# Who issues the transfers of the triangular inverses: a gated delta rule on one Trainium2 core

## The chip, the core and the metric

The kernel runs on one core of a Trainium2 chip. The metric is device microseconds (us) of that core for one execution. A NeuronCore has five engines that run side by side, each through its own queue of instructions in order: TensorE (PE in the rows, with PEld for its weight loads), VectorE (DVE), ScalarE (ACT), GpSimd (POOL) and SyncE (SP). An engine waits at the head of its queue until what the instruction needs is there, and all behind it waits too. A transfer (DMA) is issued by an instruction in the queue of one of the engines, here SyncE, ScalarE and, after the change, GpSimd; DMA engines beside them move the data.

## The reference, cut to what matters

A two-layer encoder trunk on 512 tokens of width 1024. Layer 0 mixes tokens by attention, layer 1 by a gated delta rule with eight heads; every layer has a SwiGLU block before and one behind. In the gated delta rule each head is cut into chunks, and for each chunk a unit lower triangular matrix has to be inverted:

```python
kb = k * beta[..., None]
l_mat = jnp.where(strict, jnp.einsum('bhncd,bhnsd->bhncs', kb, k) * decay, 0.0)
t_mat = lax.linalg.triangular_solve(l_mat + eye, jnp.broadcast_to(eye, l_mat.shape),
                                    left_side=True, lower=True, unit_diagonal=True)
u = jnp.einsum('bhncs,bhnsd->bhncd', t_mat, vb)
w = jnp.einsum('bhncs,bhnsd->bhncd', t_mat, kb * jnp.exp(gc)[..., None])
```

Then a scan over the chunks carries the state from one to the next.

## The kernel before, in words

All matrix work is float32, each large product as three matmuls of split operands (`wh`, `wl`: a weight panel's high and low part, `xnh`, `xnl`: the activations'). SyncE loads the weight panels, ScalarE makes `wh`, VectorE `wl`.

In the gated delta rule (`odd_mixer`, about 1330 to 1660 us of the execution) the eight heads go in four pairs. Here the chunks are 128 tokens wide, four of them. For each pair: projections to keys, queries and values (`gdn_proj`), on whose results a short convolution runs (`gdn_conv`: VectorE copies PSUM to `cx` at L924, ScalarE makes the first tap `cy` at L927, VectorE adds the other three at L929, ScalarE applies the activation, `c`); `gdn_keys` (stage `prep`) forms `iu`, the triangular matrix, at L980; `gdn_base` (stage `base`) inverts its 32x32 diagonal blocks; `gdn_head` (stage `scan`) joins these to the inverse of 128x128 and runs over the chunks; `gdn_gated` turns and gates the result `on`.

`gdn_base` is the part that the change touches. It takes a pair's two `iu` through DRAM (`iud`) so that every 32x32 block lands in one row of `lb` (four transfers, L1029), starts from the identity (`rr<-eye`, L1030), and does 31 elimination steps on GpSimd, each a product `tmp` (L1035) and a difference `rr` (L1038). Back through DRAM (`rd`, four transfers at L1041) the blocks land as `r` (two transfers, L1044). Each arrow waits for the one before: `lb` for both `iud`, the steps for all `lb`, `rd` for the last step, `r` for all `rd`. The first use of `r` is its transpose `t` on VectorE at L1053; the matmul `pb<-t,iu` on TensorE (L96) is the first that needs `t`, and it needs it of both heads.

GpSimd has one other job here: `rpow` (L160) computes small powers, `vs` in `gdn_keys` and `rs` at the end of a scan, where ScalarE's `on` (L1131) waits for it.

What stands on TensorE in which order is written by hand: `blend` merges a list of projections (the filler) with the stages, by the starts and pitches in `PLAN`, and `Ordered` keeps TensorE to the order so written. The order on the other engines is set by a scheduler that puts each instruction where it expects it to be ready.

Of the kernel before, what the change touches and what calls it, by code (L numbers as in the profile page):

```python
# [15 lines left out]
P = 128  # L16
# [85 lines left out]
class Trunk:  # L102
# [913 lines left out]
    def gdn_base(self, pool, G, Ks):  # L1016


        nc = self.nc
        n = BASE  # L1020
        iud = self.dram.tile([2 * HPITCH], F32, tag="iud", name="iud", bufs=2)
        for j, K in enumerate(Ks):
            nc.scalar.dma_start(self.rows_of(iud, j), K["iu"].rearrange("p (t s) -> p t s", s=P))
        lb = pool.tile([P, n, n], F32, tag="lb", name="lb", bufs=1)
        rr = pool.tile([P, n // 4, n], F32, tag="rr", name="rr", bufs=1)
        tmp = pool.tile([P, 9 * n], F32, tag="tmp", name="tmp", bufs=1)
        quarters = [slice(q * 2 * NBLK, (q + 1) * 2 * NBLK) for q in range(4)]
        for s in quarters:
            nc.scalar.dma_start(lb[s], self.blocks_of(iud))  # L1029
        nc.scalar.copy(out=rr, in_=G["eye"])  # L1030
        for j in range(n - 1):
            m, k = n - 1 - j, j // 4 + 1
            sh = [P, k, m]
            p = tmp[:, :k * m].rearrange("p (a b) -> p a b", b=m)
            nc.gpsimd.tensor_tensor(p, rr[:, :k, j:j + 1].broadcast_to(sh),  # L1035
                                    lb[:, j, j + 1:].rearrange("p (o m) -> p o m", o=1)
                                    .broadcast_to(sh), op=ALU.mult)
            nc.gpsimd.tensor_tensor(rr[:, :k, j + 1:], rr[:, :k, j + 1:], p, op=ALU.subtract)  # L1038
            yield
        for q, s in enumerate(quarters):  # L1040
            nc.scalar.dma_start(self.blocks_of(G["rd"], q, 4), rr[s])  # L1041
        for j, K in enumerate(Ks):
            K["r"] = pool.tile([P, T], F32, tag="r", name="r", bufs=3)
            nc.scalar.dma_start(K["r"].rearrange("p (t s) -> p t s", s=P), self.rows_of(G["rd"], j))  # L1044
        yield

    def gdn_head(self, pool, G, h, K):
# [154 lines left out]
```

## Time and profile before

| what | value |
|---|---|
| median of 3 runs | 2044.13 us (2042.98 to 2045.48) |
| the profiled execution's own time | 2044.75 us |
| its span, first to last instruction | 2042.9 us |
| mean granted clock of TensorE | 0.994 |
| busy: TensorE | 2011.8 us (98%) |
| busy: VectorE | 1086.6 us (53%) |
| busy: ScalarE | 747.5 us (37%) |
| busy: GpSimd | 129.6 us (6%) |

Times in the rows are microseconds from the span's start; "us in total, times, longest" belong to waits. A row of a timeline gives the start, the duration, the engine, the line and the operation as written <- read with its shape, and in brackets how long the engine sat idle before it and what ended that. The granted clock of TensorE is a share of full speed: 1.0 is 2.4 GHz, 0.5 is 1.2 GHz, and a value between is a mean over a stretch.

### The profile page before, as it was taken

The page shows a single profiled execution, that of the slowest core. Times are in us where ns is not written, and L with a number is a line of the kernel's source. Part 1 is how long each engine was busy: PE and PEld are TensorE (multiplying, and loading weights), DVE is VectorE, ACT ScalarE, POOL GpSimd, SP SyncE. Part 2 cuts the span into 40 slices and gives each one's busy share as a digit, 9 for nine tenths or more (in the row PEclk, how much of TensorE's full clock was granted, in tenths as well). Part 3 has the DMA queues.
Part 4 walks back from the last instruction along what each step waited for, and adds up shares of the span by engine and source line. Part 5 has one row for each costly group of instructions (what it writes and reads, how often), then busy time and mean ns, then how long its engine had stood idle before and what let it go on. Part 6 is the DMA issues. An engine that isn't in the chain of part 4 may idle for free.

```text
span 2042.9 us, 24836 instructions
## 1 busy us (share of the span) xinstructions
PE 2011.8 (98%) x9786; PEld 1669.5 (82%) x9786; DVE 1086.6 (53%) x1752; ACT 747.5 (37%) x1359; POOL 129.6 (6%) x294
## 2 busy tenths in 40 slices
PE   8999999999999999999999999998999999999998
PEld 7888888878888888888888888877877788888887
DVE  6442444587676443444544344477677675443543
ACT  5231233454663322323332123354455453322222
POOL 0000000000000000000000000005432400000000
PEclk9999999999999999999999999999999999999999
DMA  4332323222123233232332232334322333323232
GB/s 156 97 99 93 103 93 95 93 70 66 52 75 112 93 94 102 93 102 95 93 98 98 93 103 93 95 114 110 85 75 88 80 99 98 103 83 103 93 98 78
DMA packets 189866, 192.24 MB, mean 94 GB/s; under 512 B 28546, under 2 KB 165044, under 8 KB 189748
## 3 DMA queue, kind: packets, MB, share of 16 engines
q1 hardware_dynamic: 158916, 182.62, 28.5%
q10 hardware_dynamic: 30832, 8.02, 1.7%
q8 instruction: 77, 1.26, 0.3%
q14 instruction: 41, 0.34, 0.1%
HBM read 185.35 MB, written 5.26 MB: 93 GB/s over the span
## 4 chain that ended last, share of the span: by engine, by line
PE 89%; POOL 5%; DMA 2%; DVE 1%; issue 1%; ACT 1%; ACTq 0%; SPq 0%; POOLq 0%
PE mm L181 10%; PE mm L183 10%; PE mm L182 10%; PE pa L181 8%; PE pa L183 8%; PE pa L182 8%; PE pb L181 8%; PE pb L182 8%; PE pb L183 8%; PE mm L96 4%; POOL rr L1038 2%; POOL tmp L1035 2%; PE pb L96 1%; DMA lb<-iud 1%; DMA iud<-iu 1%
## 5 line engine op out<-in xcount | busy, mean ns | idle before, releaser
L175 DVE TENSOR_TENSOR wl<-raw,wh 128x1024 fp32r<-128x1024 f32 (+1 forms) x348 | 413.6, 1189 | 564.5 <-ACT wh L174 563.7
L174 ACT CAST wh<-raw 128x1024 fp32r<-128x1024 f32 (+1 forms) x348 | 355.4, 1021 | 707.5 <-PE pb L182 279.9
L181 PE MATMUL mm<-xnh,wh 128*128 128x512 f32 (+1 forms) x816 | 317.3, 390 | 0.6 <-ACT wh L174 0.6
L183 PE MATMUL mm<-xnh,wl 128*128 128x512 f32 (+1 forms) x816 | 317.8, 390 | 0.0
L182 PE MATMUL mm<-xnl,wh 128*128 128x512 f32 (+1 forms) x816 | 316.8, 389 | 0.0
L181 PEld LDWEIGHTS mm<-xnh,wh 128*128 128x128 f32 x816 | 153.9, 189 | 32.8 <-ACT wh L174 1.2
L183 PEld LDWEIGHTS mm<-xnh,wl 128*128 128x128 f32 x816 | 154.0, 189 | 32.0 <-issue 1.6
L182 PEld LDWEIGHTS mm<-xnl,wh 128*128 128x128 f32 x816 | 154.0, 189 | 30.6 <-issue 0.7
L181 PE MATMUL pa<-xnh,wh 128*128 128x512 f32 x400 | 156.3, 391 | 0.0
L183 PE MATMUL pa<-xnh,wl 128*128 128x512 f32 x400 | 155.8, 390 | 0.0
L183 PE MATMUL pb<-xnh,wl 128*128 128x512 f32 x400 | 155.8, 389 | 0.0
L181 PE MATMUL pb<-xnh,wh 128*128 128x512 f32 x400 | 155.8, 389 | 0.0
L182 PE MATMUL pb<-xnl,wh 128*128 128x512 f32 x400 | 155.8, 389 | 0.0
L182 PE MATMUL pa<-xnl,wh 128*128 128x512 f32 x400 | 155.8, 389 | 0.0
L226 ACT CAST hid<-hd 128x512 fp32r<-128x512 f32 x88 | 54.6, 620 | 209.1 <-DVE hd L398 209.1
L96 PE MATMUL mm<-xnh,wh 128*128 128x512 f32 x256 | 109.7, 428 | 11.5 <-DVE cx L924 11.5
L392 DVE TENSOR_TENSOR gr<-mm,rb 128x512 f32<-128x512 f32 x80 | 55.3, 691 | 94.7 <-PE mm L183 94.5
L182 PE MATMUL pb<-hid,wh 128*128 128x512 f32 x264 | 102.8, 389 | 0.0
L183 PE MATMUL pb<-hid,wl 128*128 128x512 f32 x264 | 102.8, 389 | 0.0
L181 PE MATMUL pa<-hid,wh 128*128 128x512 f32 x264 | 102.8, 389 | 0.0
L183 PE MATMUL pa<-hid,wl 128*128 128x512 f32 x264 | 102.8, 389 | 0.0
L181 PE MATMUL pb<-hid,wh 128*128 128x512 f32 x264 | 102.8, 389 | 0.0
(307 smaller groups left out, 3372.7 us busy)
## 6 DMA issues: line engine op xcount, KB each, us to landing
raw<-in_ffn_w_gate_dram SPq DMA_DIRECT2D x88, 512.0 KB, 3.6
raw<-in_ffn_w_up_dram SPq DMA_DIRECT2D x88, 512.0 KB, 3.5
raw<-in_ffn_w_down_dram SPq DMA_DIRECT2D x88, 512.0 KB, 3.6
raw<-in_gdn_w_in_dram SPq DMA_DIRECT2D x32, 512.0 KB, 3.9
raw<-in_att_w_in_dram SPq DMA_DIRECT2D x24, 512.0 KB, 3.5
raw<-in_gdn_w_out_dram SPq DMA_DIRECT2D x16, 256.0 KB, 2.7
xr<-in_x_dram SPq DMA_DIRECT2D x4, 512.0 KB, 5.4
raw<-in_att_w_out_dram SPq DMA_DIRECT2D x4, 512.0 KB, 3.3
```

What stands on the lines that cost most here:

```text
L96: return self.tc.keep_in_program_order(self.engine.matmul(*args, **kw))
L174: nc.scalar.copy(out=h[:, :n], in_=raw[:, :n])
L175: nc.vector.tensor_tensor(l[:, :n], raw[:, :n], h[:, :n].bitcast(F32), op=ALU.subtract)
L181: self.te.matmul(out, lhsT=lh, rhs=rh, start=start, stop=False)
L182: self.te.matmul(out, lhsT=lh, rhs=rl, start=False, stop=False)
L183: self.te.matmul(out, lhsT=ll, rhs=rh, start=False, stop=stop)
L226: nc.scalar.copy(out=h, in_=src)
L392: nc.vector.tensor_tensor(gr, g[j], self.rb, op=ALU.mult)
L1035: nc.gpsimd.tensor_tensor(p, rr[:, :k, j:j + 1].broadcast_to(sh), lb[:, j, j + 1:].rearrange("p (o m) -> p o m", o=1) .broadcast_to(sh), o ...
L1038: nc.gpsimd.tensor_tensor(rr[:, :k, j + 1:], rr[:, :k, j + 1:], p, op=ALU.subtract)
```

## The change

In `gdn_base` the four kinds of transfers are issued in GpSimd's queue instead of ScalarE's, and the copy of the identity runs on GpSimd. The two transfers that fill `rd` with zeros once, in the set-up, stay on ScalarE.

```diff
@@ -1020,14 +1020,14 @@
         n = BASE
         iud = self.dram.tile([2 * HPITCH], F32, tag="iud", name="iud", bufs=2)
         for j, K in enumerate(Ks):
-            nc.scalar.dma_start(self.rows_of(iud, j), K["iu"].rearrange("p (t s) -> p t s", s=P))
+            nc.gpsimd.dma_start(self.rows_of(iud, j), K["iu"].rearrange("p (t s) -> p t s", s=P))
...
         for s in quarters:
-            nc.scalar.dma_start(lb[s], self.blocks_of(iud))
-        nc.scalar.copy(out=rr, in_=G["eye"])
+            nc.gpsimd.dma_start(lb[s], self.blocks_of(iud))
+        nc.gpsimd.tensor_copy(rr, G["eye"])
...
         for q, s in enumerate(quarters):
-            nc.scalar.dma_start(self.blocks_of(G["rd"], q, 4), rr[s])
+            nc.gpsimd.dma_start(self.blocks_of(G["rd"], q, 4), rr[s])
         for j, K in enumerate(Ks):
             K["r"] = pool.tile([P, T], F32, tag="r", name="r", bufs=3)
-            nc.scalar.dma_start(K["r"].rearrange("p (t s) -> p t s", s=P), self.rows_of(G["rd"], j))
+            nc.gpsimd.dma_start(K["r"].rearrange("p (t s) -> p t s", s=P), self.rows_of(G["rd"], j))
```

The order of TensorE's and of SyncE's instructions stays the same, word for word. The other three change.

GpSimd, from the end of pair 0's inverse to the start of pair 1's (`vs` is the power in `gdn_keys` of pair 1; the rows with + are new):

```order
 L1035 TENSOR_TENSOR tmp<-rr,lb 128x8
 L1038 TENSOR_TENSOR rr<-rr,tmp 128x8
+L1041 DMA rd<-rr 32x8x32 x4
+L1044 DMA r<-rd 128x4x128 x2
+L1030 COPY rr<-eye 128x256
 L160 TENSOR_TENSOR vs<-sk,halfTrue 128x4 x2
+L1023 DMA iud<-iu 128x4x128 x2
+L1029 DMA lb<-iud 32x32x32 x4
 L1035 TENSOR_TENSOR tmp<-rr,lb 128x31
 L1038 TENSOR_TENSOR rr<-rr,tmp 128x31
```

All transfers of the inverse now stand between GpSimd's own instructions; for pair 1 the two `rs` of scan 0 stand between `rd` and `r`.

ScalarE, around the end of pair 0's inverse, before the change (`cy` and `c` are the convolution, `wh` a weight panel, `gosq` a sum of squares in `gdn_keys`):

```order
-L932 ACTIVATE c<-cy 128x512
-L1041 DMA rd<-rr 32x8x32 x4
-L927 ACTIVATE cy<-cx,conv 128x512
-L932 ACTIVATE c<-cy 128x512
-L174 CAST wh<-raw 128x1024
-L1044 DMA r<-rd 128x4x128 x2
-L1030 COPY rr<-eye 128x256
-L927 ACTIVATE cy<-cx,conv 128x512
-L960 ACTIVATE gosq,sk<-pa 128x128 x8
```

and what stands there now:

```order
+L932 ACTIVATE c<-cy 128x512 x2
+L927 ACTIVATE cy<-cx,conv 128x512
+L174 CAST wh<-raw 128x1024
+L927 ACTIVATE cy<-cx,conv 128x512
+L960 ACTIVATE gosq,sk<-pa 128x128 x4
```

The transfers are gone from between `c`, `cy` and `wh`.

GpSimd, in pair 3's inverse (`rs` belongs to scan 2):

```order
-L1035 TENSOR_TENSOR tmp<-rr,lb 128x48
+L160 TENSOR_TENSOR rs<-a_13064,halfFalse 128x4
+L1035 TENSOR_TENSOR tmp<-rr,lb 128x48
+L160 TENSOR_TENSOR rs<-a_13072,halfFalse 128x4
 L1038 TENSOR_TENSOR rr<-rr,tmp 128x6x8
```

The two `rs` stood thirteen steps of the inverse further down, between the last four.

## Rows read from the trace of the kernel before

**Rows 1.** The page's busy time (share of the span) and instructions of each engine.
```profile
PE 2011.8 (98%) x9786; PEld 1669.5 (82%) x9786; DVE 1086.6 (53%) x1752; ACT 747.5 (37%) x1359; POOL 129.6 (6%) x294
```
**Rows 2.** Waits of TensorE: us in total, times, longest.
```profile
PE mm L96 <- DVE cx L924: 11.5, 3, 6.1
```
**Rows 3.** Timeline of ScalarE, end of pair 0's inverse: start, us, engine, line, operation.
```profile
1424.98 1.82 ACTq L1041 DMA_DIRECT2D rd<-rr  x4
1426.89 0.72 ACT L927 ACTIVATE cy<-cx,conv 128x512 f32<-128x512 f32 x1 [11.63 <-issue]
...
1428.10 0.94 ACTq L1044 DMA_DIRECT2D r<-rd  x2
```
**Rows 4.** Timeline of ScalarE, end of pair 1's inverse.
```profile
1484.19 0.72 ACT L927 ACTIVATE cy<-cx,conv 128x512 f32<-128x512 f32 x1 [9.18 <-DMA rd<-rr]
```
**Rows 5.** Timeline of VectorE, behind pair 0's inverse.
```profile
1427.65 0.75 DVE L929 SCALAR_TENSOR_TENSOR cy<-cx,conv,cy 128x512 f32<-128x512 f32 x1 [8.69 <-ACT cy L927]
...
1433.23 0.71 DVE L1053 STREAM_TRANSPOSE t<-r 128x512 f32<-128x512 f32 x1
```
**Rows 6.** Timeline of TensorE, behind pair 0's inverse.
```profile
1429.06 0.80 PE L96 MATMUL mm<-xnh,wh 128*128 128x512 f32 x1 [6.12 <-DVE cx L924]
...
1434.30 0.39 PE L96 MATMUL mm<-xnh,wh 128*128 128x512 f32 x1
1434.53 0.39 PE L96 MATMUL mm<-xnl,wh 128*128 128x512 f32 x1
...
1438.50 0.89 PE L96 MATMUL pb<-t,iu 32*32 32x32 f32 x32
```
**Rows 7.** Timeline of TensorE, behind pair 1's inverse.
```profile
1487.53 0.80 PE L96 MATMUL mm<-xnh,wh 128*128 128x512 f32 x1 [4.83 <-DVE cx L924]
...
1491.54 0.95 PE L99 MATMUL pa<-ident,c 128*128 128x128 f32 x4
...
1497.87 0.89 PE L96 MATMUL pb<-t,iu 32*32 32x32 f32 x32
```
**Rows 8.** Windows: us, busy (instructions) of PE, PEld, DVE, ACT, POOL, clock, DMA, GB/s.
```profile
1422.90:1438.50 15.60, 9.48 (x31) 7.33 (x31) 10.01 (x23) 10.27 (x28) 4.07 (x9) 0.78 0.29 77
```
**Rows 9.** Timeline of TensorE, around the end of pair 3's inverse.
```profile
1617.51 1.25 PE L99 MATMUL pa<-ident,on 128*128 128x128 f32 x4 [2.54 <-ACT on L1131]
...
1628.45 0.89 PE L96 MATMUL pb<-t,iu 32*32 32x32 f32 x32
```
**Rows 10.** Timeline of GpSimd, near the end of pair 3's inverse.
```profile
1616.01 1.01 POOL L160 TENSOR_TENSOR rs<-a,halfFalse 128x4 f32<-128x4 f32 x1
1616.99 0.22 POOL L1038 TENSOR_TENSOR rr<-rr,tmp 128x16 f32<-128x16 f32 x1
```
**Rows 11.** Timeline of VectorE, the input of the first `rs` of rows 10.
```profile
1610.74 0.16 DVE L1127 SCALAR_TENSOR_TENSOR a<-gss,eq 128x4 f32<-128x4 f32 x1 [0.29 <-ACT gosr L1123]
```
**Rows 12.** Timeline of VectorE, the second transpose of pair 1.
```profile
1489.86 0.70 DVE L1053 STREAM_TRANSPOSE t<-r 128x512 f32<-128x512 f32 x1
```
**Rows 13.** Timelines of VectorE and TensorE, pair 2.
```profile
1550.19 0.71 DVE L1053 STREAM_TRANSPOSE t<-r 128x512 f32<-128x512 f32 x1 [0.31 <-DMA r<-rd]
...
1563.81 0.89 PE L96 MATMUL pb<-t,iu 32*32 32x32 f32 x32
```
**Rows 14.** Timeline of VectorE, both transposes of pair 3.
```profile
1625.71 1.30 DVE L1053 STREAM_TRANSPOSE t<-r 128x512 f32<-128x512 f32 x2
```
**Rows 15.** Timeline of ScalarE, start of pair 0's chain.
```profile
1383.53 0.37 ACTq L1023 DMA_DIRECT2D iud<-iu  x1
...
1385.90 2.48 ACTq L1029 DMA_DIRECT2D lb<-iud  x4
```
**Rows 16.** Groups by form, GpSimd: busy us, mean ns of one, idle before.
```profile
L160 POOL TENSOR_TENSOR rt<-ms,halfFalse 128x4 f32<-128x4 f32 x6 | 8.7, 1451 | 817.6 <-DVE ms L278 817.6
```
**Rows 17.** Windows (columns as in rows 8), pair 0's inverse in two parts.
```profile
1393.20:1419.00 25.80, 25.30 (x116) 20.70 (x115) 24.92 (x50) 14.77 (x38) 22.38 (x44) 1.00 0.40 120
1419.00:1425.00 6.00, 3.94 (x22) 3.01 (x20) 0.00 (x0) 0.00 (x0) 4.54 (x18) 1.00 0.05 17
```
**Rows 18.** Timeline of GpSimd, the first step of pair 0's inverse.
```profile
1393.25 0.56 POOL L1035 TENSOR_TENSOR tmp<-rr,lb 128x31 f32<-128x31 f32 x1 [14.79 <-DMA lb<-iud]
```

## The prediction, made before the changed kernel ran

> **What bounds the kernel now.** I read the busy shares first, then TensorE's waits, then the timelines of the engines around each wait, and last the granted clock of these stretches. TensorE is busy 2011.8 of 2042.9 us [rows 1], so only its waits, and stretches at a lower clock, can move the time. Its largest wait in the gated delta rule is for `cx`, 11.5 us in three times [rows 2]. Both long pieces of it have one cause, which the timelines show and the wait's own name does not. ScalarE issues the four `rd<-rr` transfers, which can't start until GpSimd has finished an inverse, and all that stands behind them on ScalarE stands still: before `cy` L927 it idles 11.63 us for pair 0 [rows 3] and 9.18 us for pair 1 [rows 4]. For pair 0 VectorE then idles 8.69 us before the next `cy` [rows 5], so `cx` is late and its PSUM bank is not emptied; TensorE idles 6.12 us up to 1429.06 [rows 6], and for pair 1 4.83 us up to 1487.53 [rows 7].
>
> Each wait has a second price. Twelve matmuls start between 1429.06 and 1434.30, 0.44 us apart, where the next two are 0.23 us apart [rows 6]; the granted clock of the stretch is 0.78 [rows 8], a mean of full speed (2.4 GHz) and of its half (1.2 GHz) behind the idle time. Lost: 5.24 - 12 x 0.23 = 2.5 us. After the second wait nine matmuls take 4.01 us instead of 2.07 [rows 7]; with the transposes behind them, which the half speed holds up by some 0.35 us (an estimate from their number), 2.3 us are lost.
>
> For pair 3 the wait is 2.54 us [rows 9]: the transposes of `on` need `rs`, which GpSimd runs at 1616.01 [rows 10] although its input `a` was written by 1610.90 [rows 11], since `rs` stands behind steps of the inverse in GpSimd's queue. With the same 2.3 us behind it this costs 4.8 us.
>
> **What the change removes.** No transfer of the inverse stands on ScalarE any more, so the first two waits for `cx` go: 6.12 + 2.5 and 4.83 + 2.3 us. The third goes too, 2.54 + 2.3 us, as `rs` moves thirteen steps of the inverse ahead. If nothing else were late, 21 us would be won. But the next thing on TensorE is late: `pb<-t,iu`, which needs the two transposed `r` of the pair, the end of the very chain that is moved. Without the old wait TensorE would come to it at
>
> - pair 0: 1438.50 - 8.6 = 1429.9, while the second `t` begins at 1433.23 and ends at 1433.9 [rows 5, 6];
> - pair 1: 1497.87 - 7.1 = 1490.8, while `t` ends at 1490.56 [rows 7, 12];
> - pair 2: 1563.81, while `t` ends at 1550.9: 12.9 us of slack [rows 13];
> - pair 3: 1628.45 - 4.8 = 1623.6, while `t` ends at 1627.0 [rows 9, 14].
>
> So even with transfers that cost GpSimd what they cost ScalarE, the waits partly move to `t`. From there each microsecond by which the chain from `iu` to `t` gets longer counts in full for pairs 0, 1 and 3.
>
> **What it adds to that chain.** Per pair, in series: the second `iud` issue, four of `lb`, the inverse, four of `rd`, two of `r`: eleven issues. On ScalarE they took 0.37 and 2.48 us [rows 15], 1.82 and 0.94 us [rows 3], together 5.6 us. No row shows a transfer issued by GpSimd. From below: GpSimd might hand one over in a tenth of a microsecond, and the chain would be 4.5 us shorter than now; nothing excludes that. At ScalarE's price it is as long as now. From above: a small instruction that GpSimd works through, `rs` on 128x4, takes 1.01 us [rows 10], and its costliest form `rt` 1.45 us [rows 16]. I take 1.0 us an issue, the nearest row on the engine that will do it: eleven issues are 11.0 us and the chain is 5.4 us longer (5.8 for pair 1, where the two `rs` stand between `rd` and `r` and run mostly while `rd` lands). With 1.45 us it is 10.4 us longer.
>
> The inverse itself also gets slower where VectorE stood idle beside it. From 1393.2 to 1419.0 VectorE was busy 24.92 of 25.80 us and 44 GpSimd instructions took 22.38 us, 0.51 us each; from 1419.0 to 1425.0, VectorE waiting, 18 took 4.54 us, 0.25 each [rows 17]. These are smaller steps too, so not all of it is contention. In the changed program VectorE works through the second stretch; at the first rate the 18 steps are 4.7 us dearer. I take 2 us for pair 0, 1 us for pair 1 (VectorE must have idled at the end of that inverse too, behind the same stop of ScalarE), none for pair 3.
>
> Hidden: the copy of the identity, about 0.5 us like the steps in [rows 17], runs while GpSimd waits for `lb` (14.79 us idle for pair 0 [rows 18]); were that cover gone it would cost its 0.5 us a pair. Behind the waiting `r` issues on GpSimd stand the copy, `vs` and the next pair's `iud`; the next `iu` comes from matmuls that stand behind `pb<-t,iu` in TensorE's order, so none of them is late. TensorE's and SyncE's orders don't change.
>
> **Sum.** New time of `pb<-t,iu`, with the slow matmuls behind the new wait (2.5 or 2.3 us), against now:
>
> - pair 0: 1433.9 + 5.4 + 2 + 2.5 - 1438.5 = +5.3 us
> - pair 1: 1490.6 + 5.8 + 1 + 2.3 - 1497.9 = +1.8 us
> - pair 2: the slack of 12.9 us holds 5.4 and two `rs` of 1.0; 0 us
> - pair 3: 1627.0 + 5.4 + 2.3 - 1628.45 = +6.2 us
>
> Together +13 us on the profiled execution's own 2044.75 us (span 2042.9 and 1.85 around it): 2057.8. The median of the runs shown lies 0.6 lower, at 2044.13: I predict 2057 us.
>
> **A rule weighed.** ScalarE loses far more by standing behind a transfer's wait than by issuing it: 11.63 us of idle time against 1.82 us of issue [rows 3]. The Trainium skill, "DMA: Bandwidth & Descriptors", section "Issuing engines are not separate DMA queues", says that starting transfers from several engines only saves the sequencer the time to start them, usually a small part. By that rule the change could win no more than those issues; by the row it wins the wait, if `t` is not late.
>
> **Rivals.**
>
> *A later start, no longer queue* (no difference). Issues overlap, and each of the four stages of the chain only starts a little later. Priced at 0.4 us a stage, about one `iud` issue of ScalarE [rows 15], the chain is 1.6 us longer: pair 0 +1.5; pair 1 1490.6 + 2.0 + 1 + 1.5 - 1497.9 = -2.8; pair 2 0; pair 3 1627.0 + 1.6 + 2 - 1628.45 = +2.2; sum +0.9, 2045 us. For it: a transfer's instruction may be handed on before its work is done. Against: in [rows 10] one instruction on GpSimd holds up the next. The Trainium skill, same page, section "Latency and other measured facts", gives about 1 us to the first byte on GpSimd's software path and 0.6 us on ScalarE's; no run here shows it yet, and an estimate from this page, 0.4 us more for each of four stages, would come to the same 2045 us.
>
> *GpSimd issues as cheaply as ScalarE* (faster). The chain is as long as now, and the place that wins is pair 1, where `t` then ends about when TensorE comes: pair 0 1433.9 + 2 + 2.5 - 1438.5 = -0.1; pair 1 1490.6 + 0.4 + 1 + 0.5 - 1497.9 = -5.4; pair 3 1627.0 + 1.5 - 1628.45 = 0; sum -6, 2038 us, and 2035 without contention. It decides from about 0.65 us an issue downward: there the sum crosses zero. For it: 11.63 and 9.18 us of idle time on ScalarE go for certain. Against: GpSimd's small rows.
>
> *Dearer than any row* (slower still). One `lb` issue covers 32x32 runs of 32 elements; if GpSimd's time goes by runs, an issue may be 2 us: 11 us more for each of three pairs, 2090 us.
>
> That ScalarE still stands is excluded by the new order, in which it has no transfer of the inverse.
>
> **How the numbers follow.** Forecast 0.55, dearer 0.07, later start 0.18, cheap issue 0.20. The range goes from the cheap case, 2037, to 1.45 us an issue (5 us more for three pairs), 2073. What a measurement of this kernel can tell from no change is about 0.2%, 4 us: faster 0.20, same 0.18, slower 0.62.
>
> **What would show it.** Right: ScalarE's idle times of 11.63 and 9.18 us and the `cx` waits of 6.1 and 4.8 us gone; in their place TensorE waiting for VectorE's `t` L1053, some 9, 8 and 9 us for pairs 0, 1 and 3, with a lower granted clock behind each; in GpSimd's queue transfers of about 1 us each, and 7 us or more from the last step of an inverse to the end of the second `r` issue. Wrong: issues of 0.5 us or less, or `t` in place when TensorE comes. If the part before the inverse is as long as now and only the `rd` and `r` part longer, the sum is some 6 us too high.

## The result

| | before | after |
|---|---|---|
| median of 6 runs each, on one chip | 2044.18 us (2042.95 to 2045.48) | 2056.43 us (2055.02 to 2061.3) |
| profiled execution | 2044.75 us, span 2042.9 | 2055.79 us, span 2054.0 |

The ratio is 1.006, with a 95% interval of 1.0049 to 1.0072: slower, by some 12 us. 2057 us was predicted. The sum came within a microsecond, but only one of its four terms did; that the errors of the others cancelled is luck.

### The profile page after: what moved, and what is told of

It is laid out like the page before. It is cut to its first block, busy times and chain, and to the rows that moved or that the text cites. A ratio compares the mean times of both kernels' runs of the same rounds, so it can differ in the third digit from the quotient of the medians.

```text
span 2054.0 us, 24865 instructions
## 1 busy us (share of the span) xinstructions
PE 2014.1 (98%) x9786; PEld 1671.5 (81%) x9786; DVE 1087.6 (53%) x1752; ACT 748.3 (36%) x1355; POOL 172.0 (8%) x346
## 4 chain that ended last, share of the span: by engine, by line
PE 89%; POOL 5%; DMA 2%; DVE 2%; issue 1%; ACT 1%; SPq 0%; POOLq 0%; ACTq 0%; DVEq 0%
PE mm L181 10%; PE mm L183 10%; PE mm L182 10%; PE pa L181 8%; PE pa L183 8%; PE pa L182 8%; PE pb L181 8%; PE pb L183 8%; PE pb L182 8%; PE mm L96 5%; POOL tmp L1035 2%; POOL rr L1038 2%; PE pb L96 2%; PE pb L615 1%; DVE cy L929 0%
## 5 line engine op out<-in xcount | busy, mean ns | idle before, releaser
L181 PE MATMUL pa<-hid,wh 128*128 128x512 f32 x264 | 102.7, 389 | 0.0
L182 PE MATMUL pa<-hid,wh 128*128 128x512 f32 x264 | 102.7, 389 | 0.0
```

The source lines that it names most:

```text
L181: self.te.matmul(out, lhsT=lh, rhs=rh, start=start, stop=False)
L182: self.te.matmul(out, lhsT=lh, rhs=rl, start=False, stop=False)
```

## The profile after, place by place

The page's busy time of the changed kernel answers to [rows 1]: TensorE has the same work, GpSimd 42 us more, of which the issues are most.

```profile
PE 2014.1 (98%) x9786; PEld 1671.5 (81%) x9786; DVE 1087.6 (53%) x1752; ACT 748.3 (36%) x1355; POOL 172.0 (8%) x346
```

TensorE's waits from 1340 to 1720 us (total, times, longest) answer to [rows 2]. The 11.5 us for `cx` are 1.4. What stands there instead is late for the inverse in one way or another:

```profile
PE pb L96 <- DVE kd L966: 7.9, 1, 7.9
PE pb L96 <- DVE t L1053: 7.0, 3, 5.3
PE pa L99 <- ACT vb L1013: 5.9, 1, 5.9
...
PE mm L96 <- DVE cx L923: 1.4, 1, 1.4
```

**Pair 0.** GpSimd's timeline answers to [rows 3], [rows 15] and [rows 18]: start, duration, operation, and in brackets the idle time before. The second `iud`, the four `lb`, the four `rd` and the two `r` take 0.77 + 3.15 + 2.35 + 1.54 = 7.8 us, where ScalarE took 5.6.

```profile
1383.59 0.77 POOL L1023 DMA_DIRECT2D iud<-iu  x1 [2.62 <-DVE iu L980]
1386.94 3.15 POOL L1029 DMA_DIRECT2D lb<-iud  x4 [2.58 <-DMA iud<-iu]
1394.69 0.23 POOL L1035 TENSOR_TENSOR tmp<-rr,lb 128x31 f32<-128x31 f32 x1 [4.60 <-DMA on<-gd]
...
1429.17 0.21 POOL L1038 TENSOR_TENSOR rr<-rr,tmp 128x8 f32<-128x8 f32 x1
1429.72 2.35 POOL L1041 DMA_DIRECT2D rd<-rr  x4 [0.34 <-POOL rr L1038]
1433.91 1.54 POOL L1044 DMA_DIRECT2D r<-rd  x2 [1.84 <-DMA rd<-rr]
1435.45 0.41 POOL L1030 COPY rr<-eye 128x256 f32<-128x256 f32 x1
```

VectorE and TensorE there (answering to [rows 5] and [rows 6]) stand before that result, each at the head of its own queue. TensorE's last projection begins at 1429.58, and it stops at 1437.84 - 7.88 = 1429.96; VectorE has stopped at 1427.71.

```profile
1437.08 0.71 DVE L1053 STREAM_TRANSPOSE t<-r 128x512 f32<-128x512 f32 x1 [9.37 <-DMA r<-rd]
1437.71 0.12 DVE L966 TENSOR_TENSOR kd<-br,kdc 128x4 f32<-128x4 f32 x1
...
1438.88 0.70 DVE L1053 STREAM_TRANSPOSE t<-r 128x512 f32<-128x512 f32 x1
```

```profile
1437.84 0.87 PE L96 MATMUL pb<-t,iu 32*32 32x32 f32 x16 [7.88 <-DVE kd L966]
1439.64 0.87 PE L96 MATMUL pb<-t,iu 32*32 32x32 f32 x16 [0.93 <-DVE t L1053]
```

The releaser named for the first is `kd`, a small instruction that ran directly behind `t` on VectorE; the wait is for `t`.

**Pair 1.** Not `t` but `vb` is what TensorE waits for. The chain reads from VectorE to GpSimd, ScalarE and TensorE: `a` is ready at 1482.85, but `rs` stands behind the inverse and the `rd` issues in GpSimd's queue, `on` waits for `rs`, and `vb` stands behind `on` on ScalarE. By the time TensorE reaches `pb<-t,iu`, at 1501.87, `t` is there: the second one ends at 1500.13 (answers to [rows 7] and [rows 12]).

```profile
1482.61 0.24 DVE L1127 SCALAR_TENSOR_TENSOR a<-gss,eq 128x4 f32<-128x4 f32 x1
...
1492.50 2.04 POOL L160 TENSOR_TENSOR rs<-a,halfFalse 128x4 f32<-128x4 f32 x2
...
1493.57 1.28 ACT L1131 ACTIVATE on<-on,rs 128x128 f32<-128x128 f32 x4 [5.62 <-POOL rs L160]
1494.76 1.11 ACT L1013 ACTIVATE vb<-pa,vs 128x128 f32<-128x128 f32 x4
...
1495.92 1.11 PE L99 MATMUL pa<-ident,c 128*128 128x128 f32 x4 [5.89 <-ACT vb L1013]
...
1501.87 0.89 PE L96 MATMUL pb<-t,iu 32*32 32x32 f32 x32
```

**Pair 2** wins 2.0 us that nobody had counted. In the kernel before, TensorE's transposes of `on` look like this (1.21 us for four; from the first to the next projection 0.96):

```profile
1549.39 1.21 PE L99 MATMUL pa<-ident,on 128*128 128x128 f32 x4 [0.23 <-ACT on L1131]
1550.35 0.48 PE L96 MATMUL mm<-xnh,wh 128*128 128x512 f32 x1
```

and in the changed kernel, where ScalarE no longer idles 8.04 us for `rd` ahead of them, like this:

```profile
1553.03 0.60 PE L99 MATMUL pa<-ident,on 128*128 128x128 f32 x4
1553.39 0.48 PE L96 MATMUL mm<-xnh,wh 128*128 128x512 f32 x1
```

Before, the four transposes take as long as ScalarE needs for four pieces of `on` (1.28 us for the four of pair 1): they follow it piece by piece. That the row is twice as long is not the clock: from 1549.4 to 1551.5 it is 1.00. Such a wait hardly counts as idle time (0.23 us here) and shows in the duration of a row.

**Pair 3.** GpSimd runs the two `rs` earlier (1613.93, against [rows 10]), the wait before `on` of [rows 9] is gone, and TensorE comes to `pb<-t,iu` at 1626.48, long before `t` ([rows 14]). The window's columns are those of [rows 8].

```profile
1631.82 0.87 PE L96 MATMUL pb<-t,iu 32*32 32x32 f32 x16 [5.34 <-DVE t L1053]
1633.37 0.87 PE L96 MATMUL pb<-t,iu 32*32 32x32 f32 x16 [0.68 <-DVE t L1053]
...
1648.08 0.73 PE L96 MATMUL pb<-vb,kdec 128*128 128x128 f32 x4
```

```profile
1628.00:1648.00 20.00, 15.50 (x131) 12.27 (x132) 5.28 (x13) 2.38 (x7) 1.33 (x2) 0.58 0.14 41
```

The clock of this row, 0.58, is a mean: 0.91 to 1632, while TensorE mostly stands, and 0.50 (1.2 GHz) in each quarter from there to 1648, 16 us behind the wait. From `pb<-t,iu` to the first `pb<-vb,kdec` it is 16.26 us, 15.58 of them busy; before, 1637.35 - 1628.45 = 8.90, all busy and at full clock.

How far the changed kernel is behind, by the same matmul in both traces:

| landmark on TensorE | before | after | behind | by this pair |
|---|---|---|---|---|
| `pb<-state,c`, scan of pair 0 | 1458.00 | 1460.45 | +2.45 | +2.45 |
| `pa<-ident,on` behind pair 1's start | 1515.75 | 1519.79 | +4.04 | +1.6 |
| `pb<-t,iu`, pair 2 | 1563.81 | 1565.88 | +2.07 | -2.0 |
| `pa` L274, behind the layer | 1690.76 | 1701.61 | +10.85 | +8.8 |

## The experiments

Twelve kernels, each timed in five rounds beside the kernel before (2044.3 to 2044.7 us in these sets). Unless said otherwise the edit is to the changed kernel, at 2056.4.

### Which pair loses

```diff
# gdn_base(..., p): own = p < 3
+        io = nc.gpsimd if own else nc.scalar      # for iud, lb, rd, r
+        nc.gpsimd.tensor_copy(rr, G["eye"]) if own else nc.scalar.copy(out=rr, in_=G["eye"])
```

> The changed kernel for pairs 0 to 2 alone; pair 3's transfers and its copy are ScalarE's again. Theory (pair 3's own chain, 27.55 us of inverse and a dearer chain around it, costs 8.8 us there): that goes, 2056.4 - 8.8 = about 2047.6 us, with the wait for t at 2.5 us or less in pair 3 and full clock from 1640 us on. Rival (pair 3's loss comes from what the pairs before it left, a later start of its inverse): 2054 to 2056 us. Second rival (ScalarE's own stop behind rd in pair 3, which only the old order hid): slower than 2056 us.

Measured: 2046.83 us, ratio to before 1.0015 (1.0006 to 1.0024). The theory holds: pair 3 makes 9.6 of the 12 us. Its `rs` are late again, TensorE waits 2.56 us before `on`, and then not at all for `t`; the stretch from 1628 has full clock.

```profile
1621.52 1.35 PE L99 MATMUL pa<-ident,on 128*128 128x128 f32 x4 [2.56 <-ACT on L1133]
```

```profile
1628.00:1648.00 20.00, 19.84 (x194) 16.31 (x193) 10.48 (x28) 6.65 (x24) 0.00 (x0) 1.00 0.21 57
```

So the early wait before `on`, which the prediction booked as a loss to be won back, goes with a `t` that is in time. This edit gives pair 3 both the old order and the old issues; which of the two decides is seen from `iud` and `lb` alone on ScalarE, further down. The early wait stood among projections of 512 columns and the clock was full again by 1628; the new wait stands before matmuls of 32 and 64 columns, with three projections at a time between them.

Pair 2 alone on GpSimd, with the same edit but for one line:

```diff
-        own = p < 3
+        own = p == 2
```

> The kernel before, with the transfers and the copy of pair 2 alone on GpSimd. Theory (pair 2 has 12.9 us of slack in its chain and loses ScalarE's stop of 8 us behind rd; between the ends of pair 1 and pair 2 the changed kernel won 2.0 us): about 2042 us. Rival (the 2.0 us were won back from what pair 1 had lost, not from pair 2's own edit): 2044 us, no difference. Second rival (issues on GpSimd hold up the inverse or rs of pair 2, so that the queues of pair 3 are late): 2047 us or more.

Measured: 2042.51 us, ratio 0.9996 (0.9987 to 1.0004): no difference that can be told. The trace shows the gain where the theory has it (from pair 1's `pb<-t,iu` to pair 2's 64.07 us, against 65.94 before). In the profiled execution, at 2046.68 us, more than that was lost on either side: from pair 0's `pb<-t,iu` to pair 1's 61.65 us (59.37 before), from pair 2's to pair 3's 66.77 (64.64). Whether the other runs keep part of the gain stays open.

### Which half of the chain, and the copy

```diff
-            nc.gpsimd.dma_start(self.rows_of(iud, j), ...)     # lb likewise
+            nc.scalar.dma_start(self.rows_of(iud, j), ...)
-        nc.gpsimd.tensor_copy(rr, G["eye"])
+        nc.scalar.copy(out=rr, in_=G["eye"])
```

> The changed kernel, with the first half of the chain (iud, lb, the copy of the identity) issued by ScalarE again; rd and r stay on GpSimd. Theory (the chain from iu to t sets the end, so every microsecond of issue and landing counts): in the changed kernel GpSimd issues one iud and four lb in 0.79 + 3.15 us, ScalarE did it in 0.37 + 2.48, and the landings were 0.4 + 0.3 us shorter; the first step of each inverse starts some 1.8 us earlier, pairs 0, 1 and 3 win it, 2056.4 - 5 = about 2051 us. Rival (only what stands behind the inverse matters, the first half is hidden): first steps of the inverse earlier or not, 2056 us. Second rival (ScalarE stands still again behind iud's landing, and what it makes for TensorE is late): 2058 us or more.

Measured: 2050.16 us, as the theory has it, but not for its reason. Pair 0's `pb<-t,iu` comes 1.4 us earlier, pair 1's 3.2 us later (TensorE waits 8.8 us for `vb`); what is won is pair 3's, as the table below shows. ScalarE stands still again, though no transfer that waits for the inverse is on it: the copy may not write `rr` before `rd` has been read out of it.

```profile
1431.77 0.40 ACT L1030 COPY rr<-eye 128x256 f32<-128x256 f32 x1 [12.16 <-DMA rd<-rr]
```

The same without the copy, which stays on GpSimd:

```diff
-            nc.gpsimd.dma_start(self.rows_of(iud, j), ...)
+            nc.scalar.dma_start(self.rows_of(iud, j), ...)
-            nc.gpsimd.dma_start(lb[s], self.blocks_of(iud))
+            nc.scalar.dma_start(lb[s], self.blocks_of(iud))
```

> The changed kernel, with iud and lb alone issued by ScalarE again; the copy, rd and r stay on GpSimd. With the copy on ScalarE too, the time was 2050.2 us, but the copy stood still for 12.16 us in pair 0 and 8.51 us in pair 1. Theory (the first half of the chain is some 1.8 us cheaper on ScalarE in each of three pairs): about 2051 us, with the wait for vb of pair 1 back at 4 to 6 us and that for t of pair 0 at 6 to 7. Rival (the copy's stop cost as much again in that run): 2046 us or less. Second rival (the copy's stop did no harm, and the gain of that run was the stop's, which delayed TensorE less than t does): 2056 us.

Measured: 2047.79 us, ratio 1.0018 (1.0009 to 1.0027). 8.6 us are won, more than the theory, less than the first rival, and the theory's price of 1.8 us a pair falls: the first step of pair 0's inverse is 0.94 us earlier (1393.75), its `pb<-t,iu` only 0.2 (1437.64). Nearly all of the gain is in pair 3, where the scheduler now puts `rs` two steps from the end of the inverse again (1618.71) and TensorE waits 2.55 us before `on`, not for `t`. The second `t` ends at 1629.62 + 1.48 = 1631.10 and `pb<-t,iu` begins at 1631.16: although `rd` and `r` stay on GpSimd, the early wait is just long enough. Pair 2's gain is gone: from pair 1's `pb<-t,iu` to pair 2's it is 66.10 us, with `rs` behind the inverse and the `rd` issues on GpSimd (1549.49) and `on` waiting 6.04 us for it. The kernels with one half of the chain on GpSimd and the other on ScalarE, or with `rd` and `r` on SyncE, all take 65.9 us or more here; 64.0 to 64.1 is seen only where both halves of pair 2 are on GpSimd.

The other half back on ScalarE:

```diff
-            nc.gpsimd.dma_start(self.blocks_of(G["rd"], q, 4), rr[s])     # r likewise
+            nc.scalar.dma_start(self.blocks_of(G["rd"], q, 4), rr[s])
```

> The changed kernel, with the second half of the chain (rd and r) issued by ScalarE again; iud, lb and the copy of the identity stay on GpSimd. Theory (ScalarE stands still behind rd in pairs 0 and 1, and a longer first half starts every inverse some 1.8 us later): ScalarE's idle times of some 12 and 9 us and the waits for cx of 6.1 and 4.8 us are back, each 1.8 us longer for pair 0; about 2044.2 + 1.8 + 1.8 + 1.8 = 2049 us. Rival (the first half is the cheap part, the second half makes the loss): 2044 us, as before. Second rival (both halves cost, each as dear as the whole): 2056 us.

Measured: 2054.40 us; the theory fails by 5 us. ScalarE idles 9.38 us in pair 0, as it said, but the waits for `cx` come to no more than 2.1 and 1.7 us, and pair 0 is 2.5 us better than in the changed kernel (`pb<-t,iu` at 1435.34). Pair 3 has the same loss as the changed kernel (a wait for `t` of 4.25 us), which the theory had not charged to the first half.

The copy alone, moved in the kernel before:

```diff
-        nc.scalar.copy(out=rr, in_=G["eye"])
+        nc.gpsimd.tensor_copy(rr, G["eye"])
```

> The kernel before, with the copy of the identity alone on GpSimd; all transfers stay on ScalarE. Theory (rd still stands ahead of cy on ScalarE): the idle times of some 11.6 and 9.2 us stay, no difference, 2044 us. Rival (the copy, not rd, is what holds ScalarE): they go, and the time falls to 2036 us or less. Second rival (the copy on GpSimd is in the chain): 0.4 us for each of three pairs, 2045.5 us.

Measured: 2044.34 us, ratio 1.0001 (0.9992 to 1.001), with ScalarE's 11.6 us before `cy` as they were. Copy and `rd` are two ways into one stop.

Over all kernels with the old table one number sorts pair 3, the time on TensorE from its first `pb<-t,iu` to `pa` L274:

| kernel | wait ahead of scan 3 | to `pa` L274 |
|---|---|---|
| before; pairs 0 to 2; pair 2 alone; `iud`, `lb` on ScalarE, with and without the copy; copy alone; `rd`, `r` on SyncE, with and without the copy (below) | `on`, 2.54 to 2.57 us | 62.30 to 62.35 us |
| changed | `t`, 5.34 | 69.79 |
| `rd`, `r` on ScalarE | `t`, 4.25 | 71.34 |
| `rs` on VectorE (below) | `t`, 3.98 | 69.98 |
| `lb` in eight (below) | `t`, 8.19 | 69.49 |

The span begins behind the wait: that TensorE waits there at all, 4 us or 8, costs 7 us or more after it.

### What an issue costs

`lb` in eight transfers of half the partitions each:

```diff
-            nc.gpsimd.dma_start(lb[s], self.blocks_of(iud))
+            for o in (0, NBLK):                     # half: 16 blocks of the 32
+                nc.gpsimd.dma_start(lb[s.start + o:s.start + o + NBLK], half)
```

> The changed kernel, with lb of each pair filled by eight transfers of half the partitions instead of four, all on GpSimd; the bytes are the same. Theory (an issue occupies GpSimd for about 0.79 us whatever its size, and the chain sets the end in pairs 0, 1 and 3): four issues more, 3.2 us a pair, 2056.4 + 9 = about 2065 us. Rival (an issue's time goes by its pieces, 1024 here, 512 then): the eight take as long as the four, 3.15 us, and the time is 2056 us. Second rival (the issue is hidden behind the landing of the transfer before): eight issues of 0.79, but the first step of the inverse no later than 1 us, 2058 us.

Measured: 2075.64 us, ratio 1.0156 (1.0142 to 1.017): 19 us slower, twice the theory. GpSimd's timeline of pair 0:

```profile
1383.50 2.55 POOL L1033 DMA_DIRECT2D lb<-iud  x4 [2.88 <-DMA iud<-iu]
1386.04 0.79 POOL L1023 DMA_DIRECT2D iud<-iu  x1
1389.93 2.52 POOL L1033 DMA_DIRECT2D lb<-iud  x4 [3.11 <-DMA iud<-iu]
1398.91 0.24 POOL L1039 TENSOR_TENSOR tmp<-rr,lb 128x31 f32<-128x31 f32 x1 [6.46 <-DMA lb<-iud]
```

An issue of half the size takes 0.64 us, not 0.79, so eight take 5.1 us against 3.15; the price is partly per issue, partly per piece. In pair 0 order comes on top: the second `iud` now stands behind four `lb` that wait for the first, and the inverse starts 4.2 us later. That the chain sets the end is borne out there: pair 0's `pb<-t,iu` is 5.4 us later, after a wait of 11.8. Pair 1's is 5.0 us behind the changed kernel's, pair 2's 10.3 and pair 3's 20.0 (it waits 8.19 us for `t`); in the scan of pair 2 the clock falls to 0.50 from 1583 to 1590, behind another wait of 2.16 us. How the last 15 us divide into chain, order and clock stays open.

### `rs` off GpSimd

```diff
-        self.rpow(rs, a2, NB)
+        nc.vector.reciprocal(rs, a2)
```

> The changed kernel, with rs made by VectorE as 1/a2, which leaves out the root; so GpSimd has only vs and the inverse. Theory (in pair 1 TensorE waits 5.89 us for vb, which stands behind on, which waits for rs, which stands behind the inverse in GpSimd's queue): that wait goes, TensorE comes to pb<-t,iu some 6 us earlier and waits there for t, which is only about 0.5 us earlier; pair 1 wins 1.5 us, pair 3, whose inverse holds two rs of about 1 us, wins 2: about 2053 us. Rival (the whole of the wait and the half clock behind it is won, t is not late): 2046 us. Second rival (rs has no part in it): 2056 us, and the wait for vb stays at 5.9 us.

Measured: 2058.70 us, 2 us slower than the changed kernel (this kernel leaves out the root in `rs`). The wait for `vb` is gone, so its cause is shown, and `t` takes its place at once; pair 1's `pb<-t,iu` is 2.0 us earlier. But now the wait stands directly before small matmuls, and from 1500 to 1510 the clock is 0.50 (in the changed kernel 1.00 from 1502): from there to pair 2's `pb<-t,iu` it takes 69.1 us, not 64.0.

```profile
1499.86 1.67 PE L96 MATMUL pb<-t,iu 32*32 32x32 f32 x32 [5.91 <-DVE t L1053]
```

### Without the dearer chain

The kernel before, with `rd` and `r` on SyncE:

```diff
-            nc.scalar.dma_start(self.blocks_of(G["rd"], q, 4), rr[s])     # r likewise
+            nc.sync.dma_start(self.blocks_of(G["rd"], q, 4), rr[s])
```

> The kernel before, with rd and r of all pairs issued by SyncE; iud, lb and the copy stay on ScalarE. Theory (the change took away a real loss, ScalarE's stop, and paid for it with a longer chain; the chain at the old price keeps the gain): ScalarE's idle times gone, the chain some 2 us shorter than in the changed kernel; pair 0 waits some 7 us for t, pair 1 wins some 5 us, pair 2 wins 2, pair 3 waits for t or rs as before; 2036 to 2041 us. Rival (SyncE's weight panels stand behind its wait for the inverse, 12 us in each pair, and come too late): waits of TensorE for wh or wl, 2050 us or more. Second rival (whoever issues, the inverse beside a busy VectorE is what costs): 2044 to 2048 us.

Measured: 2047.69 us, ratio 1.0015 (1.0007 to 1.0024); the theory fails. The time is that of the second rival, but its reason is not: pair 0's inverse takes 31.3 us, no longer than before. SyncE does no harm (no wait for `wh` or `wl`), but the copy on ScalarE stands in for `rd`, 12.47 us, and the waits for `cx` stay (7.3 and 5.7 us). So the copy went along, to GpSimd:

```diff
-        nc.scalar.copy(out=rr, in_=G["eye"])
+        nc.gpsimd.tensor_copy(rr, G["eye"])
```

> The kernel before, with rd and r of all pairs issued by SyncE and the copy of the identity on GpSimd; iud and lb stay on ScalarE. With rd and r on SyncE but the copy still on ScalarE, that copy stood still for 12.47 us in pair 0, since it may not write rr before the rd transfers have read it. Theory (copy and rd are two ways into the same stop, and it goes only when both leave ScalarE; the chain keeps ScalarE's and SyncE's cheaper issues): ScalarE's idle times behind an inverse gone, waits for cx gone, TensorE waits some 5 us for t in pair 0 and little in pair 1; 2036 to 2042 us. Rival (a shorter chain saves nothing, since t waits behind the inverse anyway and the half clock behind that wait eats the rest): 2044 to 2048 us. Second rival (SyncE's own stop makes weight panels late): 2050 us or more, waits for wh or wl.

Measured: 2048.89 us, ratio 1.003 (1.0019 to 1.004); slower than before, against the theory. ScalarE's stop is gone and pair 0's `pb<-t,iu` is 5.4 us earlier than before (1433.13, against 1438.50). Then pair 1 loses it: VectorE stands before `t` as ScalarE had stood before `rd`, the second head's `a` is behind `t`, and behind `a` come `rs`, `on`, `vb` and TensorE.

```profile
1490.55 0.71 DVE L1053 STREAM_TRANSPOSE t<-r 128x512 f32<-128x512 f32 x1 [9.20 <-DMA r<-rd]
1491.19 1.18 DVE L175 TENSOR_TENSOR wl<-raw,wh 128x1024 fp32r<-128x1024 f32 x1
1492.29 0.15 DVE L1127 SCALAR_TENSOR_TENSOR a<-gss,eq 128x4 f32<-128x4 f32 x1
```

```profile
1495.91 1.12 PE L99 MATMUL pa<-ident,c 128*128 128x128 f32 x4 [8.02 <-ACT vb L1013]
```

### Work for TensorE while it waits

```diff
-    ("scan", 0, 91.5, 1.91)    ("scan", 3, 260.5, 0.95)
+    ("scan", 0, 99.5, 1.66)    ("scan", 3, 266.5, 0.68)
```

> The changed kernel, with two lines of the table that sets TensorE's order: the scan of pair 0 starts 8 steps later and the scan of pair 3 six steps later, each with a shorter pitch, so that both end where they did. So projections stand on TensorE where it waited for t. Theory (the loss is TensorE standing before pb<-t,iu with half the clock behind, and nothing later is short of time): the waits of 7.9 + 0.9 us in pair 0 and 5.3 + 0.7 us in pair 3 go below 2 us each, and the stretches at half clock with them; 2056.4 - 14 to - 20, 2037 to 2043 us. Rival (the projections are missing further down, where they stood between the scan's steps): waits for pb, kdec, on or state of about the same sum there, 2054 to 2060 us. Second rival (only pair 3's half clock counts, pair 0's wait moves to pair 1): 2047 us.

Measured: 2052.17 us, ratio 1.0037 (1.0024 to 1.0049): 4 us won of 14 to 20. In pair 0 the wait for `t` is gone, and TensorE waits 6.73 us for `gy`, which empties a projection's bank and stands behind `t` on VectorE:

```profile
1438.71 0.71 DVE L1053 STREAM_TRANSPOSE t<-r 128x512 f32<-128x512 f32 x1 [9.05 <-DMA r<-rd]
...
1440.52 0.70 DVE L1053 STREAM_TRANSPOSE t<-r 128x512 f32<-128x512 f32 x1
1441.15 1.25 DVE L773 TENSOR_TENSOR gy<-mm,rb 128x512 f32<-128x512 f32 x2
```

```profile
1441.86 0.80 PE L96 MATMUL mm<-xnh,wh 128*128 128x512 f32 x1 [6.73 <-DVE gy L773]
```

The rival that named other waits was right on their kind, though they stand in the same place, not further down. In pair 3 the wait for `t` stays, 3.65 us, with the clock at 0.50 from 1632 to 1644. The last kernel joins both ideas, SyncE with the copy on GpSimd and the scans four and three steps later:

> The kernel before, with rd and r on SyncE, the copy on GpSimd, and the scans of pairs 0 and 3 four and three steps later on TensorE, with a shorter pitch, so that they end where they did. Theory (TensorE then has projections until t is there, half as far as in the version that started them eight and six steps later): some 3 to 5 us below the same kernel with the old table, 2033 to 2038 us. Rival (VectorE stands before t, and what is behind t there, cx or gy, does not empty the projections' PSUM banks, so that TensorE waits on these in place of t): no gain over the old table, 2040 to 2046 us.

Measured: 2051.74 us; the rival's side, and above its range. TensorE waits 9.49 us for `kdec`, which waits for `kd`, again behind `t` on VectorE. No kernel of this study beats the one before by what can be measured. What is left to try is `t` further down in VectorE's order, so that `a`, `kd` and `gy` go ahead of it; that wasn't tried.

## Why the prediction was right, and where it was not

The mechanism holds for pairs 0 and 3: the stops of ScalarE go, with 10 of the 11.5 us for `cx`, and the time comes back at the inverse's end, where the chain is longer. The number is in part luck: with the 2.2 us that the issues really added in place of 5.4, the prediction's own sum is +2.1 - 1.4 + 3.0 = +3.7, or 2048 us. TensorE was to come to pair 0's `pb<-t,iu` at 1429.9 and came at 1429.96. Step by step:

- **Issues, 1.0 us each: too dear.** 0.59 to 0.79 us, 7.8 us for the eleven, so +2.2 us and not +5.4. Nearest was neither `rs` on GpSimd nor the bound from ScalarE, but the middle. The "cheap" rival's turning point of 0.65 us was just missed (7.8 / 11 = 0.71). The landings, for which the sum had nothing, add some 1.2 us (medians of 2.8, 3.8, 1.9 and 3.4 us against 2.4, 3.5, 1.7 and 3.1).
- **The inverse beside a busy VectorE: too small.** From first to last step 34.7 us in pair 0 against 31.7, and 30.5 against 27.4 in pair 1: +3 each, for +2 and +1. That VectorE is the reason is argued, not shown (see the last section).
- Together the second `t` of pair 0 is 1438.88 - 1433.23 = 5.65 us later, for 7.4: the two errors cancel in part.
- **Pair 1: the wait was misnamed.** +1.6 us, for +1.8, but by `rs` behind the inverse. The prediction used that very mechanism for pair 3 [rows 10] but not for pair 1, where the same queue holds both. Its own sign of being wrong, `t` in place when TensorE comes, holds there (1500.13, for 1501.87).
- **Pair 2: 0 was predicted, -2.0 measured.** ScalarE's stop behind `rd` (8.04 us there) delays `on` and with it TensorE; the sum looked only at the slack of `t` and put this at nothing.
- **Pair 3: the step that failed most.** The second price of a wait was taken as 2.3 us wherever it stands. Behind `pb<-t,iu` 16.26 us pass in place of 8.90: 0.68 is the wait for the second `t`, and the same matmuls take 15.58 - 8.90 = 6.7 us more at half clock. So +8.8 us came for +6.2, although the second `t` ended earlier than predicted (1632.60 + 0.71, less the 2.07 from the pairs before, is 1631.2, for 1632.4).
- **Rivals.** *Later start* and *issues as cheap as ScalarE's* (2045, 2038) and *dearer than any row* (2090) are excluded by the issue's rows. What no case had is that the copy decides with the transfers; "about 0.5 us, hidden" was its cost on GpSimd, and left on ScalarE it would have kept the stop (12.16 us).
- The rule of the Trainium skill that was weighed, "DMA: Bandwidth & Descriptors", "Issuing engines are not separate DMA queues" (only the sequencer's time is saved), gives the wrong size here: a stop of 11.63 us left ScalarE, of which 1.82 us were issues [rows 3]. Yet nothing was won by that in the end, which the rule doesn't explain either.

## What to carry to other kernels

An instruction that waits for a long chain holds up its whole queue, on whichever engine it stands; take it from one and look at once for the next engine with such an instruction (here ScalarE's `rd`, ScalarE's copy, VectorE's `t`, GpSimd's `rs`, TensorE's `pb`), and for a write that must wait until the old data are read. Don't give a wait one price behind it. Here a few microseconds cost some 2 us more among projections of 512 columns, 3.1 before pair 0's scan in the changed kernel (22.61 us from `pb<-t,iu` to `pb<-state,c`, against 19.50), 5.1 before pair 1's with `rs` on VectorE, and 7 or more before pair 3's. An early short wait can be worth keeping when it lets a later, dearer one vanish.

## What the runs showed of the hardware

- **The clock behind a wait.** TensorE's granted clock was back at 1.00 within 4.5 us behind a wait of 2.54 us (the kernel before, pair 3, from 1622), within 5.2 us behind one of 6.12 us [rows 6] and within 6.2 us behind one of 7.88 us (the changed kernel, pair 0, from 1444, with six projections of 512 columns in a row). It was still at 0.50 for 16 us behind a wait of 5.34 us, with groups of small matmuls and three projections at a time behind it (the changed kernel, pair 3), and for 10 us behind one of 5.91 us (`rs` on VectorE, to 1510). So the length of the wait does not set it; what does is not shown.
- **GpSimd's issues.** 0.59 us for 32 KB in `rd`, 0.64 for 64 KB and 0.79 for 128 KB in `lb`, 0.77 for 256 KB in `iud` and `r`, against 0.46, 0.62 (128 KB) and 0.37 to 0.47 on ScalarE [rows 3, 15]. Landing took 2.8, 3.8, 1.9 and 3.4 us for `iud`, `lb`, `rd` and `r`; on ScalarE 2.4, 3.5, 1.7 and 3.1. The Trainium skill, "DMA: Bandwidth & Descriptors", "Latency and other measured facts", has about 1 us to the first byte from GpSimd and 0.6 us from ScalarE; the 0.2 to 0.4 us by which the landings differ here are that difference or less.
- **The inverse and VectorE.** In all fourteen kernels pair 0's inverse is longer where VectorE is busy longer beside it: 31.3 to 32.0 us with VectorE busy for 24.7 to 25.3 of them, 33.1 to 33.8 with 27.6 to 28.0, 34.6 to 35.4 with 29.1 to 30.8. The Trainium skill, "GPSIMD Engine Reference", "1. Specifications", says that GpSimd shares its access to SBUF with VectorE, with contention where a VectorE instruction has two inputs in SBUF or uses both ports; the order agrees. A longer inverse also holds more of VectorE's work, and no run took that work away alone, so the cause is not shown.
